# Moving the table loads and the taps' diagonal matrices around the root of the first norm

## The chip, the cores and the metric

The kernel runs on one core of a Trainium2 chip. The metric is the device time of one execution in microseconds (us), the median over several executions. The core's engines have one instruction queue each and work through it in order: PE (TensorE, matmuls), ACT (ScalarE), DVE (VectorE), POOL (GpSimd) and SP (SyncE, which here only issues DMAs).

## The reference, cut to what matters

The model is a trunk of two layers over 256 positions with 2048 channels: a Conformer convolution module, a bidirectional gated DeltaNet, and a SwiGLU feed-forward network behind each. The change lies in the first of these, between the first RMSNorm and the convolution.

```python
def rmsnorm(x, w, eps=RMS_EPS):
    y = xf * lax.rsqrt(jnp.mean(xf * xf, axis=-1, keepdims=True) + eps)
    return y * w

def conformer_conv_module(h, ...):          # h = rmsnorm(x, mix_norm[0])
    u = h @ w_pw1 + b_pw1                   # 2048 -> 4096
    a, gate = jnp.split(u, 2, axis=-1)
    u = a * jax.nn.sigmoid(gate)
    u = depthwise_conv_centred(u, w_dw) + b_dw      # 31 taps over positions
    u = jax.nn.silu(layernorm(u, ln_g, ln_b))
    return u @ w_pw2 + b_pw2
```

## The kernel before, in words

Activations lie transposed: a tile is 128 channels by 256 positions, so the 2048 channels are 16 tiles, k = 0 to 15. A weight matrix is streamed from DRAM in tiles `raw` of 128 x 1024 (eight blocks of 128 x 128); `halves` splits each half of such a tile into two reduced-precision parts, `hi` (a cast on ACT, line 181) and `lo` (a subtraction on DVE, line 182). `products` multiplies: in the first projection each block gives three matmuls, `hi` with the high and with the low part of the activations (lines 211 and 212) and `lo` with the high part (line 213). A product of one 128-channel output thus needs 16 x 3 = 48 matmuls, two `raw` tiles and four `hi`/`lo` pairs. The tag `hi` has four buffers, `raw` three, and the accumulators (tag `lin`) three PSUM banks.

The first norm is not applied before the projection. `norm_tile` scales each input tile by the norm's weight, splits it (`xs`, lines 263 and 264), squares it on ACT (`sq`, line 273) and adds the squares on DVE (`ss`, line 280). The factor that is missing, one over the root of the mean square, is worked out while the first products run: `token_sum` adds `ss` over the partitions with a matmul against a matrix of ones (`tsum`, line 286), `rsqrt` takes the root on ACT (line 297) and its reciprocal on DVE (line 301, `rstd`). `norm_end` only stores this as `self.pending`; `products` runs it at its end, for output j = 0.

The loop over j = 0 to 15 then makes, for each output tile, two products (value `pa` and gate `pg`; for j = 0 both together, in two of the three `lin` banks; afterwards one after the other). DVE multiplies both by `rstd` (`ta`, line 364, and `tg`, line 368), which frees their banks; ACT takes the sigmoid of `tg` (line 369), DVE joins them in `up` (line 370). The 31 taps of the convolution over `up` are shared out: some on PE, as matmuls with a diagonal matrix per tap (`diag`, made on ACT from the identity matrix, line 382; sixteen buffers), eleven on ACT and POOL (lines 395, 396), the rest on DVE (line 404). A diagonal matrix depends on constants alone, not on the input.

The order of each engine's queue is laid out ahead of the run by a scheduler that plays the program through with its own times for instructions and transfers. It takes, of what is ready in its play, the instruction of the highest priority. The weight splits stand highest of what is used here (`WP` = 800), then the norm (`HP` = 550), then the rest in the order of the program. `tc.issue_after(x)` keeps the instructions traced in its block behind x in their engine's queue, without a wait for x to finish. The order is fixed when the kernel runs. ACT evaluates functions from a table, and a change of function can need a load of another table, which is an instruction of its own (ACT_TABLE_LOAD) put ahead of the first instruction that needs it. `warm(func, after)` runs a function on one column of a tile, so that the load stands there.

Of the kernel before, what the change touches and what calls it, by code (L numbers as in the profile page):

```python
# [7 lines left out]
F32 = mybir.dt.float32  # L8
F32R = mybir.dt.float32r
AF = mybir.ActivationFunctionType  # L10
# [3 lines left out]
P = 128  # L14
S = 256
D = 2048
# [25 lines left out]
NDIAG = 16  # L42
# [40 lines left out]
class Trunk:  # L83
# [169 lines left out]
    def norm_tile(self, k, wname, wi, prep=True, first=None):  # L253
        nc = self.nc
        h = self.h[k]
        w = self.p(wname, wi + k)
        if prep:
            xs = self.xp.tile([P, 2 * S], F32R, tag=f"xs{k}", name=self.nm(f"xs{k}"))
            if first and k == 0:

                t = nc.scalar.activation(self.ss, h, AF.Square)
            with self.tc.issue_after(t.ins) if first and k == 0 else nullcontext():
                nc.scalar.activation(xs[:, :S], h, AF.Copy, scale=w)
            nc.vector.scalar_tensor_tensor(  # L264
                xs[:, S:], h, w, xs[:, :S].bitcast(F32), op0=ALU.mult, op1=ALU.subtract)
            self.xs[k] = xs
        sq = self.ss
        if self.ss_n:
            sq = (first or self.sp).tile([P, S], F32, tag="m" if first else "sq", bufs=4 if first else 1, name=self.nm("sq"))
        last = not prep and k == KD - 1  # L270
        if first:
            if k:
                nc.scalar.activation(sq, h, AF.Square)
        else:
            (nc.vector if last else nc.gpsimd).tensor_tensor(sq, h, h, op=ALU.mult)  # L275
        self.rest = sq if last else None
        if last:
            self.warm(AF.Sqrt, self.ss)
        elif self.ss_n:
            (nc.vector if first else nc.gpsimd).tensor_tensor(self.ss, self.ss, sq, op=ALU.add)  # L280
        self.ss_n += 1
# [12 lines left out]
    def rsqrt(self, src, scale, eps, then=None, out=None):  # L294
        nc = self.nc
        r = self.sp.tile([P, S], F32, tag="rstd", bufs=2, name=self.nm("rstd"))
        nc.scalar.activation(r, src, AF.Sqrt, scale=scale, bias=eps)
        if then is not None:
            self.warm(then, r)
        out = r if out is None else out  # L300
        nc.vector.reciprocal(out, r)
        return out

    def norm_end(self):

        ss = [self.ss] if self.rest is None else [self.ss, self.rest]
        self.pending = lambda: self.rsqrt(self.token_sum(*ss), 1.0 / D, self.c("eps6"))

    def conv_module(self, next_norm):
        nc, tc, sp = self.nc, self.tc, self.sp
        self.new_h()
        self.load_first([self.pw1[0], self.pw1[KD]])
        with tc.tile_pool(name="conv", bufs=1, reuse_waits="tile") as cv:
            self.norm_begin()
            with tc.high_priority(HP):
                for k in range(KD):
                    self.norm_tile(k, "mixn", 0, first=cv)
            self.norm_end()  # L320
            xs = self.xs
            new = lambda tag, bufs: cv.tile([P, S], F32, tag=tag, bufs=bufs, name=self.nm(tag))
            half = TAPS // 2
# [31 lines left out]
            for j in range(KD):  # L355
# [11 lines left out]
                with tc.high_priority(LAST if j == KD - 1 else 0):  # L367
                    nc.vector.tensor_tensor(tg, pg, rstd, op=ALU.mult)
                    nc.scalar.activation(tg, tg, AF.Sigmoid, bias=self.p("bpw1", KD + j))
                    nc.vector.scalar_tensor_tensor(u, ta, self.p("bpw1", j), tg, op0=ALU.add, op1=ALU.mult)  # L370

                    w = lambda t: wdw[:, j * TAPS + t : j * TAPS + t + 1]
                    x = lambda t: up[:, t : t + S]
                    acc = new(f"a{j}", 1)
                    npe, npool = NPE[j], NPOOL[j]
                    own = None
                    if j == KD - 1:
                        own = self.ps.tile([P, S], F32, tag="b", bufs=PSB["b"], name=self.nm("own"))
                    diags = []
                    for t in range(2, 2 + npe):  # L380
                        g = cv.tile([P, P], F32, tag="diag", bufs=NDIAG, name=self.nm("diag"))
                        nc.scalar.activation(g, self.mat("ident"), AF.Copy, scale=w(t))
                        diags.append(g)

                    r = [self.ps.tile([P, S], F32, tag=g, bufs=PSB[g], name=self.nm("r")) for g in ("b", "g")]
                    for n, g in enumerate(diags):
                        nc.tensor.matmul(r[0], g, x(2 + n), start=(n == 0), stop=(n == npe - 1))
                    if j < SHIFTED:
                        nc.scalar.activation(r[1], x(1), AF.Copy, scale=w(1))
                    else:  # L390
                        nc.vector.scalar_tensor_tensor(r[1], x(1), w(1), shift, op0=ALU.mult, op1=ALU.subtract)
                    nc.scalar.activation(acc, x(0), AF.Identity, scale=w(0), bias=self.p("bdw", j))
                    for t in range(2 + npe, 2 + npe + npool):
                        m = new("m", 4)
                        scaled = nc.scalar.activation(m, x(t), AF.Copy, scale=w(t))  # L395
                        nc.gpsimd.tensor_tensor(acc, acc, m, op=ALU.add)  # L396

                    rs = (own, r[1]) if own else r
                    for n, t in enumerate(range(2 + npe + npool, TAPS)):
                        o = rs[n % 2]  # L400
                        if n == 0 and own:
                            nc.vector.tensor_scalar(o, x(t), w(t), None, op0=ALU.mult)
                        else:
                            nc.vector.scalar_tensor_tensor(o, x(t), w(t), o, op0=ALU.mult, op1=ALU.add)
                    if own:
                        self.more, self.five, self.more_raw = cv, 0, 2
                        with tc.issue_after(self.raw_dma.ins):
                            raws = [self.raw_weights(self.pw2[c], 0, CK) for c in range(FIRSTS)]
                        pre = [None] * FIRSTS

                        def highs(c):
                            r = raws[c][:, : CS * P]
                            hi, lo = (cv.tile([P, CS * P], F32R, tag=t, bufs=XB, name=self.nm(t)) for t in ("hi", "lo"))
                            nc.scalar.copy(hi, r)
                            pre[c] = (r, hi, lo)
                            return hi

                        def weights(c, after=None):

                            r, hi, lo = pre[c]  # L420
                            with tc.issue_after(after.ins) if after else nullcontext():
                                nc.vector.tensor_tensor(lo, r, hi.bitcast(F32), op=ALU.subtract)
                            pre[c] = [(hi[:, x * P : (x + 1) * P], lo[:, x * P : (x + 1) * P]) for x in range(CS)]

                        with tc.issue_after(scaled.ins):
                            self.warm(AF.Sqrt, tg)
                            for c in range(PRE):
                                pre_hi = highs(c)
                    if own:

                        part = new("part", 1)
                        nc.vector.tensor_copy(part, own)
                        for o in (r[1], r[0]):
                            nc.vector.tensor_tensor(part, o, part, op=ALU.add)
                        t = nc.vector.tensor_tensor(acc, acc, part, op=ALU.add)
                        weights(0, t)
                        weights(1, t)
                    else:
                        for o in r:
                            nc.vector.tensor_tensor(acc, acc, o, op=ALU.add)  # L440
# [725 lines left out]
```

## Time and profile before

| | |
|---|---|
| time, median of 3 runs | 2806.75 us |
| lowest and highest | 2803.21 and 2806.95 us |
| profiled execution, its time | 2802.27 us |
| profiled execution, its span | 2800.5 us |
| PE busy in the span | 2754.0 us, 98% |
| ACT and DVE busy in the span | 1759.7 us (63%) and 2065.2 us (74%) |
| mean granted clock of TensorE | 0.998 |

The span runs from the first to the last instruction of the profiled execution, and its own time is 1.77 us longer. That execution is faster than the median by 4.48 us. Times inside the trace count from the span's start. A busy time of PE counts overlapping matmuls, so that its share says where it waited more than how well it was used.

### The profile page before, as it was taken

The numbers are of one execution on the slowest core, as the hardware profiler recorded it, in microseconds if no ns is written. First come the engines' busy times: TensorE is split into PE (matmuls) and PEld (weight loads), VectorE is DVE, ScalarE is ACT, GpSimd is POOL, SyncE is SP. The second block draws the span as 40 slices with busy tenths as digits, with TensorE's granted clock in tenths as the row PEclk, the third lists the DMA queues.
The fourth block names the chain that finished last, engine by engine and source line by source line (L and its number), as shares of the span: only waits on it lengthen the run. The fifth ranks groups of instructions, "written<-read, shape, count | busy, mean of one in ns | idle before, by whom it ended". The sixth has DMA issues, their size and how long they took to land.

```text
span 2800.5 us, 50212 instructions
## 1 busy us (share of the span) xinstructions
PE 2754.0 (98%) x18224; PEld 2510.1 (90%) x18224; DVE 2065.2 (74%) x3892; ACT 1759.7 (63%) x3716; POOL 367.9 (13%) x427
## 2 busy tenths in 40 slices
PE   8999999999999999999999999999999999999998
PEld 7998888888888889999999999998888888888887
DVE  8999876666666667889898989856666666665555
ACT  8877555555554445776978878765455555555443
POOL 3764310000000112000000000001110000000111
PEclk9999999999999999999999999999999999999999
DMA  5443565555556665776565665576666655566664
GB/s 188 137 146 127 179 202 189 189 189 190 191 188 194 198 199 176 237 235 201 174 231 168 227 197 193 182 254 189 190 209 190 191 189 188 189 189 187 189 191 139
DMA packets 170649, 532.88 MB, mean 190 GB/s; under 512 B 18944, under 2 KB 42752, under 8 KB 170400
## 3 DMA queue, kind: packets, MB, share of 16 engines
q1 hardware_dynamic: 169104, 528.37, 59.3%
q8 instruction: 143, 2.34, 0.3%
q10 hardware_dynamic: 1296, 1.30, 0.1%
q14 instruction: 106, 0.87, 0.1%
HBM read 500.69 MB, written 28.90 MB: 189 GB/s over the span
## 4 chain that ended last, share of the span: by engine, by line
PE 82%; ACT 6%; DVE 4%; DMA 4%; issue 2%; POOL 2%; SPq 0%; POOLq 0%; DVEq 0%; ACTq 0%
PE acc L207 39%; PE acc L206 20%; PE acc L213 5%; PE acc L212 5%; PE acc L211 5%; POOL a L396 2%; DVE lo L182 2%; PE psa L925 1%; PE psb L967 1%; ACT hi L181 1%; DMA raw<-in_win 1%; PE psb L990 1%; PE acc L209 1%; DMA raw<-in_wout 1%; PE psg L778 1%
## 5 line engine op out<-in xcount | busy, mean ns | idle before, releaser
L182 DVE TENSOR_TENSOR lo<-raw,hi 128x512 fp32r<-128x512 f32 x1759 | 1256.3, 718 | 641.6 <-ACT hi L181 634.3
L181 ACT CAST hi<-raw 128x512 fp32r<-128x512 f32 x1759 | 1076.3, 619 | 835.2 <-PE acc L207 658.4
L207 PE MATMUL acc<-xs,hi 128*128 128x512 f32 x2816 | 967.3, 392 | 0.0
L206 PE MATMUL acc<-xs,lo 128*128 128x256 f32 x2640 | 744.1, 282 | 0.0
L207 PEld LDWEIGHTS acc<-xs,hi 128*128 128x128 f32 x2816 | 517.0, 188 | 99.0
L211 PE MATMUL acc<-xs,hi 128*128 128x256 f32 x2064 | 585.7, 285 | 13.7 <-ACT hi L181 8.9
L213 PE MATMUL acc<-xs,lo 128*128 128x256 f32 x2064 | 586.5, 285 | 2.8 <-DVE lo L182 2.7
L212 PE MATMUL acc<-xs,hi 128*128 128x256 f32 x2064 | 585.0, 284 | 1.1 <-DVE xs L264 1.0
L206 PEld LDWEIGHTS acc<-xs,lo 128*128 128x128 f32 x2640 | 498.4, 189 | 8.4
L207 PE MATMUL acc<-hs,hi 128*128 128x512 f32 x1408 | 486.8, 391 | 0.0
L211 PEld LDWEIGHTS acc<-xs,hi 128*128 128x128 f32 x2064 | 389.6, 189 | 18.6 <-ACT hi L181 10.5
L213 PEld LDWEIGHTS acc<-xs,lo 128*128 128x128 f32 x2064 | 389.6, 189 | 11.9 <-issue 5.7
L212 PEld LDWEIGHTS acc<-xs,hi 128*128 128x128 f32 x2064 | 390.3, 189 | 6.6 <-issue 4.1
L206 PE MATMUL acc<-hs,lo 128*128 128x256 f32 x1376 | 388.3, 282 | 0.0
L207 PEld LDWEIGHTS acc<-hs,hi 128*128 128x128 f32 x1408 | 262.4, 188 | 52.8
L206 PEld LDWEIGHTS acc<-hs,lo 128*128 128x128 f32 x1376 | 260.1, 189 | 1.6
L532 POOL TENSOR_TENSOR tg<-tg,rstd 128x256 f32<-128x256 f32 x88 | 65.4, 744 | 905.6 <-ACT tg L531 905.6
L207 PE MATMUL acc<-ys,hi 128*128 128x512 f32 x512 | 177.7, 392 | 0.0
L396 POOL TENSOR_TENSOR a<-a,m 128x256 f32<-128x256 f32 x171 | 150.3, 880 | 97.3 <-ACT m L395 85.3
L206 PE MATMUL acc<-ys,lo 128*128 128x256 f32 x496 | 140.3, 284 | 2.2 <-DVE lo L182 2.2
L275 POOL TENSOR_TENSOR sq<-h 128x256 f32<-128x256 f32 x59 | 53.4, 905 | 543.4 <-DVE h L543 384.5
L711 DVE SCALAR_TENSOR_TENSOR u<-t,par_sb,u 128x254 f32<-128x254 f32 (+1 forms) x256 | 120.3, 480 | 2.3 <-ACT u L707 1.8
(239 smaller groups left out, 2910.1 us busy)
## 6 DMA issues: line engine op xcount, KB each, us to landing
raw<-in_gu SPq DMA_DIRECT2D x352, 512.0 KB, 4.5
raw<-in_win SPq DMA_DIRECT2D x194, 512.0 KB, 4.4
raw<-in_dn SPq DMA_DIRECT2D x160, 512.0 KB, 3.6
raw<-in_pw SPq DMA_DIRECT2D x94, 512.0 KB, 3.8
raw<-in_wout SPq DMA_DIRECT2D x64, 512.0 KB, 4.4
a_d<-am SPq DMA_DIRECT2D x32, 512.0 KB, 4.3
ar<-a_d SPq DMA_DIRECT2D x32, 512.0 KB, 5.0
raw<-in_dn SPq DMA_DIRECT2D x32, 256.0 KB, 3.6
```

The source lines that it names most:

```text
L181: nc.scalar.copy(hi, r)
L182: nc.vector.tensor_tensor(lo, r, hi.bitcast(F32), op=ALU.subtract)
L206: nc.tensor.matmul(acc[:, S:], lo, a[:, :S], start=False, stop=False)
L207: nc.tensor.matmul(acc, hi, a, start=first, stop=last)
L209: nc.tensor.matmul(acc[:, S:], lo, a[:, :S], start=False, stop=False)
L211: nc.tensor.matmul(acc[:, :S], hi, a[:, :S], start=first, stop=False)
L212: nc.tensor.matmul(acc[:, :S], hi, a[:, S:], start=False, stop=False)
L213: nc.tensor.matmul(acc[:, :S], lo, a[:, :S], start=False, stop=last)
L275: (nc.vector if last else nc.gpsimd).tensor_tensor(sq, h, h, op=ALU.mult)
L396: nc.gpsimd.tensor_tensor(acc, acc, m, op=ALU.add)
L532: nc.gpsimd.tensor_tensor(tg, tg, rstd, op=ALU.mult)
L711: nc.vector.scalar_tensor_tensor(u[:, lo:hi], t[:, lo + s : hi + s], w(i), u[:, lo:hi], op0=ALU.mult, op1=ALU.add)
```

## The change

Four things are different. `norm_tile` remembers the last tile of squares, and the conv module runs a one-column Sqrt on that tile behind the sixteenth input tile, inside the norm's priority block. `norm_end` takes a function and hands it to `rsqrt`, and the conv module gives it Sigmoid. `rsqrt` remembers its root instruction and runs that function on one column of the constants instead of one column of the root's result, behind the root in the queue. The taps' diagonal matrices are put behind the root in ACT's queue.

```diff
         if first:
             if k:
                 nc.scalar.activation(sq, h, AF.Square)
+            self.squared = sq
...
     def rsqrt(self, src, scale, eps, then=None, out=None):
...
-        nc.scalar.activation(r, src, AF.Sqrt, scale=scale, bias=eps)
+        self.root = nc.scalar.activation(r, src, AF.Sqrt, scale=scale, bias=eps)
         if then is not None:
-            self.warm(then, r)
+            with self.tc.issue_after(self.root.ins):
+                self.warm(then, self.cst)
...
-    def norm_end(self):
+    def norm_end(self, then=None):
...
-        self.pending = lambda: self.rsqrt(self.token_sum(*ss), 1.0 / D, self.c("eps6"))
+        self.pending = lambda: self.rsqrt(self.token_sum(*ss), 1.0 / D, self.c("eps6"), then)
...
                 for k in range(KD):
                     self.norm_tile(k, "mixn", 0, first=cv)
-            self.norm_end()
+                self.warm(AF.Sqrt, self.squared)
+            self.norm_end(AF.Sigmoid)
...
-                    for t in range(2, 2 + npe):
-                        g = cv.tile([P, P], F32, tag="diag", bufs=NDIAG, name=self.nm("diag"))
-                        nc.scalar.activation(g, self.mat("ident"), AF.Copy, scale=w(t))
-                        diags.append(g)
+                    with tc.issue_after(self.root.ins):
+                        for t in range(2, 2 + npe):
+                            g = cv.tile([P, P], F32, tag="diag", bufs=NDIAG, name=self.nm("diag"))
+                            nc.scalar.activation(g, self.mat("ident"), AF.Copy, scale=w(t))
+                            diags.append(g)
```

In the kernel before, no caller gave `rsqrt` a function, so that its `warm` did not run. The other norms still give none.

## Rows read from the trace of the kernel before

**Rows 1.** The page, busy time of each engine over the span.

```profile
PE 2754.0 (98%) x18224; PEld 2510.1 (90%) x18224; DVE 2065.2 (74%) x3892; ACT 1759.7 (63%) x3716; POOL 367.9 (13%) x427
```

**Rows 2.** Busy time by stretch: from:to, length, busy of each engine (instructions), clock, DMA.

```profile
40.00:250.00 210.00, 207.03 (x1570) 199.36 (x1568) 198.92 (x381) 168.44 (x395) 151.08 (x170) 1.00 0.45 145
250.00:300.00 50.00, 45.64 (x234) 37.57 (x235) 45.61 (x107) 38.17 (x78) 6.59 (x10) 1.00 0.39 132
300.00:2790.00 2490.00, 2473.22 (x16242) 2247.78 (x16240) 1787.78 (x3337) 1519.89 (x3169) 206.01 (x231) 1.00 0.61 195
```

**Rows 3.** Timeline of PE, 23 to 37 us: start, length, instruction, idle before.

```profile
23.47 0.70 PE L286 MATMUL tsum<-ss,cst_sb 128*128 128x256 f32 x2
25.20 0.39 PE L211 MATMUL acc<-xs,hi 128*128 128x256 f32 x1 [1.04 <-ACT hi L181]
25.43 0.28 PE L212 MATMUL acc<-xs,hi 128*128 128x256 f32 x1
25.93 0.39 PE L213 MATMUL acc<-xs,lo 128*128 128x256 f32 x1 [0.22 <-DVE lo L182]
...
31.16 0.28 PE L212 MATMUL acc<-xs,hi 128*128 128x256 f32 x1
31.28 0.28 PE L213 MATMUL acc<-xs,lo 128*128 128x256 f32 x1
34.27 0.55 PE L211 MATMUL acc<-xs,hi 128*128 128x256 f32 x1 [2.71 <-DVE ta L364]
...
37.15 0.28 PE L212 MATMUL acc<-xs,hi 128*128 128x256 f32 x1
```

**Rows 4.** Busy time by stretch, the slow matmuls alone (columns as in rows 2).

```profile
34.27:37.15 2.88, 2.88 (x13) 2.88 (x14) 1.51 (x4) 0.63 (x2) 0.00 (x0) 0.51 0.71 205
```

**Rows 5.** Timeline of ACT, 21 to 35 us.

```profile
21.32 0.41 ACT L273 ACTIVATE sq<-h 128x256 f32<-128x256 f32 x1
21.62 3.02 ACT L382 ACTIVATE diag<-cst_sb,wdw 128x128 f32<-128x128 f32 x10
24.55 1.12 ACT L181 CAST hi<-raw 128x512 fp32r<-128x512 f32 x2
25.57 1.86 ACT L382 ACTIVATE diag<-cst_sb,wdw 128x128 f32<-128x128 f32 x6
27.34 1.13 ACT L181 CAST hi<-raw 128x512 fp32r<-128x512 f32 x2
28.49 1.28 ACT L297 ACT_TABLE_LOAD   x1
29.78 0.47 ACT L297 ACTIVATE rstd<-tsum,cst_sb 128x256 f32<-128x256 f32 x1
30.15 2.17 ACT L181 CAST hi<-raw 128x512 fp32r<-128x512 f32 x4
32.34 1.28 ACT L369 ACT_TABLE_LOAD   x1
34.48 0.51 ACT L369 ACTIVATE tg<-tg,par_sb 128x256 f32<-128x256 f32 x1 [0.86 <-DVE tg L368]
```

**Rows 6.** Timeline of DVE, 21 to 35 us.

```profile
21.94 1.48 DVE L280 TENSOR_TENSOR ss<-ss,sq 128x256 f32<-128x256 f32 x3
...
30.29 1.75 DVE L301 RECIPROCAL rstd<-rstd 128x256 f32<-128x256 f32 x1 [1.01 <-ACT rstd L297]
31.96 1.83 DVE L182 TENSOR_TENSOR lo<-raw,hi 128x512 fp32r<-128x512 f32 x3
33.70 0.42 DVE L364 TENSOR_TENSOR ta<-acc,rstd 128x256 f32<-128x256 f32 x1
```

**Rows 7.** Timeline of SP, issues of weight tiles behind the first ones.

```profile
14.27 0.65 SPq L168 DMA_DIRECT2D raw<-in_pw  x1
...
19.52 0.93 SPq L168 DMA_DIRECT2D raw<-in_pw  x2
```

**Rows 8.** Tile raw, issue to landing: issues at 13 to 15 us, at 19 to 21.

```profile
DMA to landing us min/median/max: 7.4/7.4/7.4
...
DMA to landing us min/median/max: 4.6/5.0/5.3
```

**Rows 9.** Line 292, a one-column warm on a tile in SBUF: duration min/median/max in ns.

```profile
L292 ACT ACTIVATE warm<-rstd x1: 203/203/203, 263.3 to 263.3; 128x1 f32<-128x1 f32 x1
```

## The prediction, made before the run

> **What bounds the kernel now.** I read the page first. PE is busy 98% of the span [rows 1], so a change on ACT can pay only where PE waits for ACT, directly or through another engine. Then the busy time by stretch: from 40 to 250 us PE is busy 207.0 of 210 us and from 300 to 2790 us 2473 of 2490 [rows 2]. What PE gains ahead of 40 us should therefore reach the end, and there is little else to win. The change acts between the last square and the first sigmoid, so I read PE's timeline there for gaps. The reader is to see two. Behind the token sum, at 24.17 us, PE waits until 25.20 for a cast and is held up again until 25.93 by its low part. Then the next product runs at a step of 0.12 us a matmul, and behind its last one, started at 31.28, nothing starts until 34.27, when `ta` has freed a PSUM bank [rows 3]. Behind this gap the granted clock is 0.51, the 1.2 GHz level, for 2.88 us and 13 matmuls [rows 4]. Behind the shorter gap the step soon is 0.12 us, so it cost no clock.
>
> ACT's and DVE's timelines say who is late. ACT runs ten diagonal matrices straight after the last square, from 21.62 us, then two casts, six more diagonals, two casts, and only then the table load and the root at 29.78 [rows 5], though the token sum was there at 24.17 [rows 3]. The root is 5.6 us late. The reciprocal ends at 32.04, three `lo` follow, then `ta` at 33.70 [rows 6]; that is PE's wait. And the cast that PE lacks at 24.17 stands behind ten diagonals, while its `raw` tile, issued at 14.27, landed 7.4 us later, about 21.7 [rows 7, 8].
>
> **The change part by part.** What follows takes the queue order that I think likeliest: squares, Sqrt load and warm, casts 1 and 2, root, Sigmoid load and warm, casts 3 and 4, then diagonals between later casts. The scheduler lays the order anew; the other orders are rivals below.
>
> First, the Sqrt load moves behind the last square. Load 1.28 us [rows 5], from 21.62 to 22.90; warm 0.20 [rows 9], to 23.1. Nobody waits meanwhile: DVE adds the last squares until 23.42 [rows 6], PE has its token sum until 24.17. The warm reads a square that ACT itself has just written.
>
> Second, the diagonals leave the stretch from 21.62 to 24.64. Casts 1 and 2 run at 23.1 to 24.2 (1.12 us, rows 5), their `lo` from 23.7 on at 0.65 each (three take 1.83 with overlap, rows 6), so until 24.4 and 25.0. The two token-sum matmuls overlap in 0.70 us; a matmul can follow at about 24.0 rather than 25.20: 1.2 us. Matmul three came 0.38 late (0.50 instead of 0.12, rows 3); now it must wait for 24.4 instead of 24.24, 0.17. Gain here: 1.2 + 0.38 - 0.17 = 1.4 us.
>
> Third, the root runs at 24.2 to 24.7, as soon as the sum is there, and the reciprocal behind `lo` 2, 25.0 to 26.75 (1.75, rows 6). PE ends the running product (48 matmuls, 5.6 us at 0.117) at about 30. To avoid the gap, `ta` (0.42) must be through by then. Even with three `lo` ahead of it, as now, which wait for casts 3 to 5, I get 29.0 to 29.8. The gap goes: 34.27 - 31.28 - 0.12 = 2.87 us. With it goes the slow clock: 13 matmuls in 2.88 us instead of 13 x 0.117 = 1.52, so 1.36 us.
>
> Fourth, the Sigmoid load moves ahead of casts 3 and 4. It costs nothing today, for ACT then waits 0.86 us for `tg` [rows 5]. In its new place it runs 24.7 to 26.0, warm to 26.2, cast 3 to 26.8, its `lo` behind the reciprocal to 27.5. PE wants that cast at 24.0 + 24 x 0.117 = 26.8 plus the 0.17, and its `lo` by 27.2: a loss of 0.3 us. The second pair of transfers, issued from 19.52 and landing within 5.3 us, is there by 25.4 [rows 7, 8] and not what is late. No tie to the root's tile means only that the warm need not wait for the root's end; ACT works in order, so this is worth nothing to 0.1 us.
>
> Fifth, the 16 diagonals, 3.02 + 1.86 = 4.9 us of ACT [rows 5], come back behind the root. They hide in idle ACT time: 40 to 250 us has 41 us of it [rows 2]. Five are wanted for j = 0, the others for later tiles. The two warms add 0.4 us, covered likewise. If that cover is missing, the price is the last rival. The number of table loads stays the same.
>
> Sum: 1.4 + 2.87 + 1.36 - 0.3 = 5.3 us. From the profiled execution, 2802.27 becomes 2797.0; that execution lies 4.5 us under the median of the runs, so I forecast 2806.75 - 5.3 = 2801.5 us. Bounds: if only the second gap goes, and half of the clock loss, 3.5; if new waits are nil, 5.6. What the new order does downstream no row shows; PE's remaining waits bound the good side, 3.0 us from 40 to 250 and 4.4 from 250 to 300 [rows 2], and I take nothing of either.
>
> A rule to weigh: the table load at 28.49 begins 0.02 us behind the cast and the root starts 0.01 us behind the load; the same holds ahead of the second load [rows 5]. A switch costs ACT 1.28 us here and no more. The Trainium skill ("ScalarE: Activation LUTs", section "What ACT_TABLE_LOAD costs") gives 1.28 us for the load and 1.38 more for a drain, 2.66 a switch. The trace does not agree with the drain; by that figure the forecast would be some 3.6 us of gain.
>
> **The rivals.** (a) The Sigmoid load ends up ahead of casts 1 and 2: root and Sigmoid warm are laid in front of them, because the scheduler's own transfer times may have `raw` later than it really is (ten diagonals found room ahead of the cast). Against it: a cast outranks the root once ready. Then the casts begin at 26.2, PE stands from 24.0 to 26.9 and likely loses the clock, 1.36. The product ends 1.36 + 5.65 later, at 33.9, but `ta` is long ready. Before, the next product began at 34.27 and lost 1.36 itself: net gain 1.7, 2805.0 us.
>
> (b) The gain is made but partly lost from 40 to 300 us. DVE is busy 199 of 210 us there [rows 2], so work that arrives earlier does not all run earlier, and one more wait for `lo` in another order goes to PE. Price, up to as much again as PE waits there now, 3 us, and with a bad end of the module 5: 2803.8 to 2806.8.
>
> (c) The new order also closes some of those waits: 2 to 4 us more, 2797.5 to 2799.5.
>
> (d) Each table switch holds ACT for longer in the new place than the load row says, by a drain that the present neighbours hide: at 1.28 us more (taken as one load again) cast 1 is 1.2 us late and cast 3 1.5 more, gain 3.6 to 3.0 us, 2803.2 to 2803.8. This is where the rule above would lead; the 0.01 us gaps speak against it.
>
> (e) Slower: the diagonals are laid in one block between the Sigmoid warm and cast 3. The cast then starts at 26.2 + 4.9 = 31.1, its first user on PE at 31.75 instead of 27.0: 4.7 us of standstill and 1.36 of clock, 6.1 against the 5.65 won: 0.4 us slower, 2807.2, more if the next casts slip as well. It decides from 15 diagonals in front of that cast. For it: they are ready at once. Against it: the cast's rank, and today six diagonals, not sixteen, fit between these casts.
>
> **How the numbers follow.** Forecast 52%, own range 2800.0 to 2803.3. (a) 12%, (b) 14%, (c) 14%, (d) 3%, (e) 5%. The likeliest gives 2801.5. The range 2797.5 to 2807.0 leaves out the upper half of (e), a tail of (c), and unmodelled noise of the median, whose three runs lie 3.7 us apart. This kernel can be told from no change by about 0.2%, 5.6 us, which is 2801.1: the sum stops just short of it. Faster by more: all of (c) and 24 of the forecast's 52, 38%. Slower by more: a worse (e) or (b), 6%. Between: 56%.
>
> **What would show it.** In the changed trace: a load behind the last square at about 21.6 us, casts from 23.1, the root by 24.7, no `diag` ahead of it; the second load under line 292 directly behind the root, none under line 369; PE without a wait for `ta` and at full clock from 31 to 37 us, and the first convolution matmul some 5 us earlier than now. Wrong would be the sum if PE waits over 1 us for a cast between 24 and 40 us, if `ta` still comes later than 30, or if PE's busy time from 40 to 300 us falls by several us for the same instructions.

## The result, and the profile after

The changed kernel takes 2815.63 us (median of 6 runs, 2814.62 to 2817.82), the kernel before 2805.1 us in 6 runs (2800.54 to 2807.57). The ratio is 1.0040, with a 95% interval of 1.0028 to 1.0052: about 11 us slower, where 5.3 us faster was forecast. The profiled execution took 2814.62 us, over a span of 2812.8.

The first question is where the time line moves. Each matmul of PE has its counterpart in the other trace (same line of the code, same tiles). The median difference of their start times, in a few us around a place, gives how far the kernel is ahead there (minus) or behind (plus): -0.8 us at 18 us, ahead of the change; -5.1 at 45; -4.9 at 240; still -5.2 at 1290. Then the DeltaNet stage is run, and at 1910 us it is +12.6, which stays so to the end (+12.3). So the first norm wins 4 to 5 us, close to what was forecast, and a stage that the diff does not touch, 1250 us later, loses 17.8 in this execution.

The next view is the busy time by stretch, with the borders put on the same matmuls. First the kernel before, then the changed one. The columns are those of [rows 2].

```profile
0.00:1290.00 1290.00, 1267.44 (x8144) 1147.88 (x8145) 969.32 (x1792) 807.20 (x1634) 255.75 (x306) 1.00 0.59 186
1290.00:1910.00 620.00, 608.57 (x5038) 586.63 (x5037) 531.51 (x1164) 483.48 (x1243) 28.12 (x16) 1.00 0.62 203
```

```profile
0.00:1284.80 1284.80, 1266.67 (x8143) 1146.24 (x8144) 967.55 (x1793) 807.78 (x1637) 255.36 (x306) 1.00 0.59 187
1284.80:1922.50 637.70, 615.99 (x5037) 594.81 (x5036) 532.53 (x1164) 487.07 (x1242) 24.91 (x17) 0.98 0.61 197
```

The middle stretch has the same work, 5037 matmuls on PE, and grows from 620.0 to 637.7 us. PE is idle 637.7 - 616.0 = 21.7 us in it instead of 11.4, which is 10.3 us, and it is busy 7.4 us longer with the same matmuls, since the clock is lower: 0.98 instead of 1.00.

The first norm itself is in ACT's timeline, which answers to [rows 5]:

```profile
21.05 1.14 ACT L181 CAST hi<-raw 128x512 fp32r<-128x512 f32 x2
22.21 1.28 ACT L293 ACT_TABLE_LOAD   x1
23.50 0.20 ACT L293 ACTIVATE warm<-sq 128x1 f32<-128x1 f32 x1
23.70 2.42 ACT L181 CAST hi<-raw 128x512 fp32r<-128x512 f32 x4
26.10 0.48 ACT L298 ACTIVATE rstd<-tsum,cst_sb 128x256 f32<-128x256 f32 x1
26.60 1.28 ACT L293 ACT_TABLE_LOAD   x1
27.89 0.20 ACT L293 ACTIVATE warm<-cst_sb 128x1 f32<-128x1 f32 x1
28.00 4.19 ACT L386 ACTIVATE diag<-cst_sb,wdw 128x128 f32<-128x128 f32 x14
32.10 0.60 ACT L181 CAST hi<-raw 128x512 fp32r<-128x512 f32 x1
...
33.71 0.51 ACT L372 ACTIVATE tg<-tg,par_sb 128x256 f32<-128x256 f32 x1
```

Both loads stand where the diff puts them, and the root starts at 26.10 instead of 29.78. Six casts, not two, run ahead of it, and the diagonals come in a block of fourteen. PE's token sum has moved too, from 23.47 us [rows 3] to a place among the products, and it ends at 26.06, so that the root could not have run earlier:

```profile
25.47 0.59 PE L287 MATMUL tsum<-ss,cst_sb 128*128 128x256 f32 x2
```

On DVE the reciprocal and `ta` follow at once, where three `lo` stood between them [rows 6]:

```profile
26.84 1.75 DVE L303 RECIPROCAL rstd<-rstd 128x256 f32<-128x256 f32 x1
28.62 0.42 DVE L367 TENSOR_TENSOR ta<-acc,rstd 128x256 f32<-128x256 f32 x1
```

And of PE's two gaps [rows 3] these waits are left between 18 and 45 us (total, times, longest):

```profile
PE acc L211 <- DVE ta L367: 0.6, 1, 0.6
PE acc L211 <- ACT hi L181: 0.5, 1, 0.5
PE acc L212 <- DVE xs L264: 0.2, 1, 0.2
PE acc L213 <- DVE lo L182: 0.2, 1, 0.2
```

The wait for `xs`, at 19.73 us, lies ahead of the change; the kernel before has it too, with 0.27 us.

The granted clock of that stretch no longer falls, where it was 0.51 before [rows 4]:

```profile
24.00:37.00 13.00, 11.73 (x92) 11.04 (x91) 9.19 (x16) 12.83 (x33) 0.00 (x0) 1.00 0.46 153
```

### The profile page after: what moved, and what is told of

The parts are those of the page before. It is cut to its first block, busy times and chain, and to the rows that moved or that the text cites. A ratio compares the mean times of both kernels' runs of the same rounds, so it can differ in the third digit from the quotient of the medians.

```text
span 2812.8 us, 50213 instructions
## 1 busy us (share of the span) xinstructions
PE 2760.6 (98%) x18224; PEld 2515.7 (89%) x18224; DVE 2063.8 (73%) x3892; ACT 1763.5 (63%) x3718; POOL 364.1 (13%) x427
## 4 chain that ended last, share of the span: by engine, by line
PE 83%; ACT 5%; DVE 5%; DMA 3%; issue 2%; POOL 2%; SPq 0%; POOLq 0%; DVEq 0%; ACTq 0%
PE acc L207 40%; PE acc L206 20%; PE acc L213 5%; PE acc L212 5%; PE acc L211 5%; POOL a L400 2%; PE psa L929 2%; DVE lo L182 1%; DMA raw<-in_win 1%; PE psb L994 1%; PE psb L971 1%; ACT hi L181 1%; PE acc L209 1%; PE psg L782 1%; ACT m L399 1%
## 5 line engine op out<-in xcount | busy, mean ns | idle before, releaser
L211 PEld LDWEIGHTS acc<-xs,hi 128*128 128x128 f32 x2064 | 390.2, 189 | 16.4 <-ACT hi L181 10.2
```

Source lines behind the costliest of these rows:

```text
L211: nc.tensor.matmul(acc[:, :S], hi, a[:, :S], start=first, stop=False)
```

## What differs in the DeltaNet stage

The queue orders of the two kernels can be set side by side, for the order is fixed when the program is made. PE's queue differs in the first norm and the start of the convolution, then no more through the rest of the convolution and the first FFN, and again from the DeltaNet stage on. From the second FFN to the end it is the same once more. The first place where PE differs in the DeltaNet stage is this, with the kernel before ahead and the changed kernel below (in the first list line 1042, in the second line 1046 is the transposition of a value tile):

```
before:  L213 (k = 6)   L1042 psg x2             L211 L212 L213 (k = 7)
after:   L213 (k = 6)   L211 L212 L213 (k = 7)   L1046 psg x2
```

Two transposes come three matmuls later. From there on the orders of PE, DVE, ACT and SP drift apart until the stage's end. One thing that this does is seen at 1490 to 1545 us of the changed kernel. ACT:

```profile
1492.61 1.15 ACT L181 CAST hi<-raw 128x512 fp32r<-128x512 f32 x2 [2.41 <-DMA raw<-in_win]
1496.77 0.62 ACT L181 CAST hi<-raw 128x512 fp32r<-128x512 f32 x1 [3.02 <-DMA raw<-in_win]
1497.29 5.02 ACT L910 COPY pb<-w 32x512 f32<-32x512 f32 x8
1502.32 1.66 ACT L910 COPY bl<-pd 32x256 f32<-32x256 f32 x4
1503.99 2.92 ACT L825 ACTIVATE stk<-xd 32x256 f32<-32x256 f32 x8
1506.93 0.47 ACT L787 ACTIVATE kk<-psg,rt 128x256 f32<-128x256 f32 x1
1507.30 1.51 ACT L937 COPY z<-psa 32x256 f32<-32x256 f32 x4
```

and PE, with the stretch's busy time and clock:

```profile
1508.87 2.93 PE L929 MATMUL psa<-w,z 128*128 128x64 f32 x16 [3.98 <-ACT z L937]
```

```profile
1495.00:1545.00 50.00, 46.02 (x374) 45.82 (x374) 35.63 (x77) 41.19 (x97) 1.95 (x1) 0.93 0.46 158
```

Casts stand in ACT's queue ahead of twenty small copies and wait for weights, twice, 5.4 us in all. The copies and `z` slip behind them, and PE, which works in order, waits 3.98 us for `z`. Behind that wait the clock is down: 0.50, the 1.2 GHz level, from 1509.8 to 1516.4 us, and 0.93 over the 50 us, where the kernel before has 1.00 from 1500 to 1550.

```profile
1509.80:1516.40 6.60, 6.60 (x33) 6.60 (x33) 6.50 (x14) 6.20 (x15) 0.00 (x0) 0.50 0.51 159
```

In the kernel before, the eight `pb` copies of the same step start right behind a cast that waited for nothing, seven us earlier, and the copies to `z` start at 1499.99 instead of 1507.30:

```profile
1489.62 0.61 ACT L181 CAST hi<-raw 128x512 fp32r<-128x512 f32 x1
1490.13 5.02 ACT L906 COPY pb<-w 32x512 f32<-32x512 f32 x8
...
1499.99 1.53 ACT L933 COPY z<-psa 32x256 f32<-32x256 f32 x4
```

Over the stage, the changed kernel's two largest waits of PE are for `lo` and for `z`. These are the same two rows in the kernel before, where three other waits are larger (2.3, 2.1 and 1.7 us), and then in the changed kernel:

```profile
PE acc L206 <- DVE lo L182: 1.3, 2, 1.0
...
PE psa L925 <- ACT z L933: 0.6, 1, 0.6
```

```profile
PE acc L206 <- DVE lo L182: 5.8, 2, 3.0
PE psa L929 <- ACT z L937: 5.3, 2, 4.0
```

## The experiments

The theories: by the **order theory** the first norm's part gains what its rows show, and the loss is the order of the DeltaNet stage's queues. The scheduler lays it out anew when its plan arrives there a fraction of a microsecond earlier or later, and it does not matter what moved the plan. By the **shift theory** the stage loses because its work really arrives 5 us earlier, in whatever order. By the **parts theory** the loads, the warms or the diagonals cost it.

A means to part them: matmuls put into the first FFN, whose result nobody reads, move the scheduler's plan without touching either stage. NUDGE is their number, NCOLS is 256. No experiment leaves out work of the kernel before.

```diff
                 tg, tu, hf = new("tg"), new("tu"), new("hf")
+                if layer == 0 and j == 2:
+                    nudge = self.ps.tile([P, 512], F32, tag="g", bufs=PSB["g"], name=self.nm("nudge"))
+                    for n in range(NUDGE):
+                        nc.tensor.matmul(nudge[:, :NCOLS], xs[0][:, :P], xs[0][:, :NCOLS], start=True, stop=True)
```

The time lines of all runs, by the same measure as above (us ahead or behind the kernel before, in one profiled execution each). At 18 us all stand between -0.2 and -0.8 already, so that much of each figure is the start of that execution. The DeltaNet column is the difference of the two columns before it. "Order" names the DeltaNet stage's order on PE, as the traces show it; B is that of the kernel before, A that of the changed one.

| kernel | order | at 240 us | at 1290 | at 1910 | DeltaNet | ratio (95% interval) |
|---|---|---|---|---|---|---|
| changed | A | -4.9 | -5.2 | +12.6 | +17.8 | 1.0040 (1.0028 to 1.0052) |
| e1: before, 2 matmuls | A | -0.6 | -0.2 | +18.2 | +18.4 | 1.0063 (1.0050 to 1.0077) |
| e2: changed, 28 matmuls | B | -5.0 | +2.8 | +6.1 | +3.3 | 1.0003 (0.9994 to 1.0011) |
| e3: changed, one tap moved | B | -4.5 | -4.8 | -2.9 | +1.9 | 0.9989 (0.9980 to 0.9997) |
| e4: both loads, diagonals as before | D | +0.2 | +1.1 | +8.5 | +7.4 | 1.0030 (1.0021 to 1.0039) |
| e5: diagonals alone | A | -3.0 | -2.5 | +14.9 | +17.4 | 1.0034 (1.0021 to 1.0046) |
| e6: sigmoid's load alone | B | -1.0 | -0.7 | -1.4 | -0.7 | 0.9999 (0.9990 to 1.0008) |
| e7: before, 1 matmul | E | -0.5 | +0.3 | +10.2 | +9.9 | 1.0022 (1.0013 to 1.0032) |
| e8: changed, 8 matmuls | C | -5.3 | -4.1 | +6.0 | +10.1 | 1.0007 (0.9998 to 1.0015) |

A profiled execution can lie off its kernel's median: e8's is 3.4 us above it, e5's 2.9 us. If the difference of the medians, less the column at 1290, is taken for the DeltaNet column, it reads from the top +15.7, +18.2, -1.3, +1.5, +7.3, +12.7, +0.6, +6.7 and +5.4 us. Order B then stands within 1.5 us of the kernel before, and the four others are 5 to 18 us slower.

**e1, the kernel before with NUDGE = 2.** 

> The kernel before, with two more matmuls (128x256, result read by nobody) in the first FFN; the first norm is untouched. Laid out by the scheduler, its queues have the same order as before up to the DeltaNet stage, and in that stage the order of the changed kernel, instruction for instruction. Order theory (the change's loss is the DeltaNet stage's order, which the scheduler lays anew for any small shift of its plan): that stage is 17.2 us longer as in the changed kernel, plus 0.25 us for the matmuls: 17.5 us slower, ratio 1.006. Shift theory (the stage loses because its work arrives 5 us earlier at run time) and parts theory (the loads and diagonals cost it): 0.25 us, ratio 1.000.

It took 2820.94 us against 2802.93: 18 us slower, for 0.25 us of work in another stage and without a letter of the change. In its trace the stage has the length and the waits of the changed kernel (lines are shifted by two):

```profile
1289.80:1928.10 638.30, 617.31 (x5037) 595.96 (x5036) 532.26 (x1165) 486.94 (x1243) 24.70 (x16) 0.98 0.59 197
```

```profile
PE psa L931 <- ACT z L939: 6.0, 2, 4.3
PE acc L208 <- DVE lo L184: 5.8, 2, 3.4
```

The shift theory and the parts theory both wanted no difference here. The loss comes without an earlier arrival and without the parts, so neither is needed for it.

**e2, the changed kernel with NUDGE = 28.** 

> The changed kernel, with 28 such matmuls in the first FFN. Its queues have the changed kernel's order in the first norm and the convolution, and in the DeltaNet stage the order of the kernel before. Order theory: 4.9 us won ahead of the FFN as read in the changed kernel's trace, 28 x 0.117 = 3.3 us given for the matmuls, DeltaNet as before: 1.6 us faster, ratio 0.9994. Shift theory: DeltaNet's work still comes 1.6 us earlier than before, so some loss up to 17 us: 0 to 15 us slower. Parts theory: as the changed kernel and 3.3 us more, 13.8 us slower, ratio 1.005.

2804.40 us, ratio 1.0003; the order theory's 0.9994 is just the lower end of the interval, and the parts theory's 1.005 is far outside. The shift theory's 0 to 15 us slower is not excluded by this run. Its profiled execution (2809.34 us) is the slowest of its twelve runs and shows the clock at 0.93 from 1300 to 1350 us in the same order B in which the kernel before has 1.00. So some us of its +3.3 belong to that execution. Nor are the 28 matmuls all of the way from -5.0 at 240 us to +2.8 at 1290: at 410 us, behind them, the run stands at -0.3, and between 1150 and 1250 us it loses 3.1 us more, where PE's order is the same in both kernels.

**e3, the changed kernel with one tap of tile 1 off PE.**

```diff
 NDIAG = 16
+NPE[1] = 4
+NPOOL[1] = 12
```

> The changed kernel, with one tap of convolution tile 1 moved from PE to ACT and POOL (two matmuls of 0.22 us each and one diagonal less, one scaled copy and one POOL addition more). By the scheduler's layout the DeltaNet stage has the order of the kernel before, without added work. Order theory: 4.9 us from the first norm and 0.4 us from the tap: 5.3 us faster, ratio 0.998. Shift theory: the work comes 5.3 us earlier, so the loss stays: about 10 us slower. Parts theory: 10 us slower.

2799.66 us against 2802.93, ratio 0.9989 with an interval below 1: faster than both kernels, by 3.3 us where 5.3 was expected. The stretch ahead of the stage is 4.8 us shorter than before, as in the changed kernel, and the stage is back near its old length:

```profile
0.00:1285.20 1285.20, 1266.45 (x8141) 1146.45 (x8142) 968.83 (x1792) 807.93 (x1636) 257.52 (x307) 1.00 0.56 187
1285.20:1907.00 621.80, 609.95 (x5037) 589.50 (x5036) 531.74 (x1164) 484.80 (x1243) 27.58 (x16) 0.99 0.60 202
```

The tap gave nothing that the trace shows (-4.5 at 240 us, against -4.9 without it): what it does is to bring back order B. The shift theory is refuted a second time, for here the work arrives early too.

**e4, both loads moved, the diagonals not tied.**

```diff
-                    with tc.issue_after(self.root.ins):
+                    with nullcontext():
                         for t in range(2, 2 + npe):
```

> The changed kernel with the diagonal matrices not tied behind the root (both table loads moved as in the change). Its queues in the first norm are those of the kernel before but for the two loads, so PE's two gaps should be there still: at most 1.3 us won, for the root's load is no longer ahead of it. Its DeltaNet stage has a third order, that of neither kernel. Order theory: that stage is off from before by anything from some us faster to 17 us slower, and the first norm's gain stays under 1.5 us. Parts theory with the diagonals as the cost: the 17 us loss is gone. Parts theory with the loads as the cost: it stays, 15 to 17 us slower.

2811.37 us, 8.4 us slower, and the first norm wins nothing (+0.2 at 240 us). ACT's timeline shows why: without the tie the diagonals still stand ahead of the first casts, and now around the load as well, so the root starts at 29.63, as late as before.

```profile
21.36 3.02 ACT L386 ACTIVATE diag<-cst_sb,wdw 128x128 f32<-128x128 f32 x10
24.28 1.12 ACT L181 CAST hi<-raw 128x512 fp32r<-128x512 f32 x2
25.31 0.40 ACT L386 ACTIVATE diag<-cst_sb,wdw 128x128 f32<-128x128 f32 x1
25.73 1.28 ACT L293 ACT_TABLE_LOAD   x1
...
27.13 1.26 ACT L386 ACTIVATE diag<-cst_sb,wdw 128x128 f32<-128x128 f32 x4
28.30 1.12 ACT L181 CAST hi<-raw 128x512 fp32r<-128x512 f32 x2
...
29.63 0.45 ACT L298 ACTIVATE rstd<-tsum,cst_sb 128x256 f32<-128x256 f32 x1
```

Neither form of the parts theory has 8.4 us: it wanted the whole loss or none of it.

**e5, the diagonals alone** (both `warm` calls left out of the changed kernel). 

> The kernel before with only the diagonal matrices tied behind the root; no table load is moved by hand. By its layout PE's queue is that of the changed kernel throughout, the DeltaNet stage's too. Order theory: as the changed kernel within 2 us, 8.5 to 12.5 us slower, with 4 to 5 us won in the first norm. Parts theory with the loads as the cost: the gain without the loss, 4 to 5 us faster.

2815.07 us, 10.2 us slower than the kernel before in that job, like the changed kernel. At 45 us it is 4.6 us ahead (0.2 of it at 18 us already), so the tie alone wins the 4 to 5 us that I expected in the first norm. By 240 us only 3.0 are left, for PE waits again at 54 and 70 us, for `lo`, where the changed kernel has no such wait:

```profile
PE acc L213 <- DVE lo L182: 1.3, 2, 1.0
```

Its root starts at 27.96 instead of 26.10, behind a cast that waited 1.37 us for a transfer and behind the load, and DVE's work up to there runs later. In these two executions the loads by hand are thus worth 1 to 2 us beside the tie, behind the norm and not in it, and none of the loss.

**e6, the sigmoid's load alone.** 

> The kernel before with only the sigmoid's load put directly behind the root. By its layout all of PE's queue is that of the kernel before, in the DeltaNet stage too. Order theory: no difference beyond 1 us (the casts behind the load are 0.2 us later by the warm). Parts theory with this load as the cost: slower by several us.

Ratio 0.9999. With order B kept, nothing is lost.

**e7, the kernel before with NUDGE = 1.** 

> The kernel before with one additional matmul in the first FFN, 0.12 us. The first norm is untouched; the DeltaNet stage comes out in a fourth order, that of none of the kernels run so far. Order theory: the stage is off by anything from some us faster to 18 us slower, and the rest of the time line within 1 us of before. Shift theory and parts theory: no difference, ratio 1.000.

2811.84 us, 7.0 us slower for 0.12 us of work. With e1 this shows that the layout of the stage, and not the matmuls, sets its time.

**e8, the changed kernel with NUDGE = 8.** 

> The changed kernel with eight such matmuls in the first FFN, 0.9 us; the first norm's order is the changed kernel's, the DeltaNet stage comes out in a fifth order. Order theory: 4.0 us won ahead of the DeltaNet stage, and the stage off from before by anything from some us faster to 18 us slower. Shift theory: as the changed kernel plus 0.9, 11 us slower.

2806.16 us, ratio 1.0007: 9 us better than the changed kernel by the two ratios, although it does more. The shift theory's 11 us are refuted a third time.

## Why the prediction was wrong, point by point

**The gaps and their cause** were right. The root was late for the diagonals, and so was the cast. With the tie the root starts 3.7 us earlier, the wait for `ta` falls from 2.71 to 0.56 us, and the 13 matmuls at half clock are gone.

**The sum of the first norm** was 5.3 us; the time line shows 4.9 at 240 us (5.1 at 45), of which 0.8 stood at 18 us already, so 4.1 to 4.3. The difference lies in the terms for the new waits. I had 0.3 for one late `lo`; there are 0.56 for `ta`, 0.49 for a cast behind the block of diagonals and 0.22 for its `lo`, 1.3 in all, and 5.3 - 1.0 = 4.3 is what is found. The root did not come behind two casts but behind six, at 26.10 instead of my 24.2, and the token sum that it needs, which I left where it was, moved from 24.17 to 26.06 (its end).

**Rival (e)** happened in its form and not in its price: fourteen diagonals were laid in one block ahead of a cast, and PE lost 0.49 us by it instead of 4.7, because four more casts had been laid ahead of the block.

**The load** costs 1.28 us in its new places too: the warm at 23.50 begins 0.01 us behind the load, and the second load 0.02 us behind the root. Rival (d) is out. The Trainium skill ("ScalarE: Activation LUTs", section "What ACT_TABLE_LOAD costs") adds a drain of 1.38 us to each switch; neither of these two loads shows one.

**The step that failed** is the one from the first norm to the end: "What PE gains ahead of 40 us should therefore reach the end", with nothing taken for the new order downstream. From PE's 98% I concluded that nothing would be lost on the way. PE's remaining idle time bounds only what could still be won, not what a new order can cost. The DeltaNet stage kept PE at 608.6 of 620 us in one particular order, and four other orders of the same work that ran here lost 5 to 18 us by the medians, 15.7 us in the changed kernel. All that the prediction named as signs of a wrong sum lay ahead of 300 us. Rival (b) had the mechanism, a new order downstream, but looked for it from 40 to 300 us and priced it by the idle time of the old order, at 5 us at most. (Its times, 2803.8 to 2806.8, are 2.3 to 5.3 us above the forecast and do not follow from its prices of 3 and 5; nothing else hangs on this.) And 6 in 100 for slower was far too little for a queue layout that nothing in the rows held in place.

**What stays open.** Why the scheduler's plan tips in this stage when it arrives a little earlier or later, and not in the FFNs, no run here shows. Nor was it measured how much each of the stage's waits costs by itself; the wait for `z` is the clearest example, not the whole 17.8 us. And e3's gain of 3.3 us is smaller than its time line ahead of the stage; the 1.9 us that its stage was longer in order B lie within what one order varies by (e6: -0.7, e2: +3.3).

## What to carry to other kernels

Where a scheduler lays out the queues from a simulated time line, an edit is two changes: the one that was written, and a new layout of every stage that sits near a tie. Before a local gain of a few us is carried to the end, compare the queue orders of the two programs stage by stage; a stage that the diff does not touch but whose order differs is a term of the sum with both signs, sized by what other orders of it have cost and not by its idle time. If the local part is good and the far order bad, move the plan by something harmless until the good order returns, as e3 does, or pin the order of that stage, which was not tried here.

## What the runs showed of the hardware

A wait can cost twice in a stage that keeps PE full. In the changed kernel's DeltaNet stage 10.3 us more of PE's idle time came with 7.4 us more busy time for the same 5037 matmuls, at a mean clock of 0.98 instead of 1.00. The plainest case is the wait for `z`: PE stands idle 3.98 us until 1508.87, and from 1509.8 to 1516.4 us its matmuls run at a granted clock of 0.50, the 1.2 GHz level.

Not every wait does so: in this stage PE was idle for 11.4 us in the kernel before, and its clock stayed at 1.00. Single executions of one order differ too. E2's profiled execution had 0.93 from 1300 to 1350 us, where the kernel before had 1.00 in the same order. That execution of the kernel before stands high, with a mean clock of 0.998; its executions beside e1 to e8 have 0.993 to 0.998, the changed kernel's six 0.992 to 0.995. So the 7.4 us are read from one pair of executions, and how much of the medians' 10.5 us is clock was not measured.
